# Twelve of 22 down-projection groups by Strassen instead of eleven, and seven of them prepared during the up projection instead of five

## The chip, the cores and the metric

The kernel runs on one core of a Trainium2 chip. Its metric is device time in microseconds. Three runs of the kernel before gave 1444.36, 1444.54 and 5140.6 us; the median, 1444.54 us, is what the prediction is compared with.

Five engines matter: TensorE (PE in the profile, with its weight loads as PEld), VectorE (DVE), ScalarE (ACT), and the queues from which DMAs are issued: SP's for nearly all of them, ACT's for a few. Every engine works through its own instructions strictly in the order in which they were written into the program; semaphores make one wait for another.

## The reference

One block of a streaming encoder on 256 tokens of width 2048, in float32: two token mixers (multi-scale mean pooling, multi-scale retention) merged by gates, and a gated feed-forward layer of width 5632. The change touches the feed-forward layer alone:

```python
def conv_glu(h, w_up, conv_w, conv_b, w_down):
    ug = h @ w_up                                  # (256, 2048) @ (2048, 11264)
    gate, up = ug[..., :D_FF], ug[..., D_FF:]      # D_FF = 5632
    gate = causal_depthwise_conv3(gate, conv_w) + conv_b
    return (jax.nn.silu(gate) * up) @ w_down       # (256, 5632) @ (5632, 2048)
```

## The kernel before

**Precision.** A float32 product is made of three matmuls on reduced-precision operands: each operand is split into a high part `hi` and a rest `lo`, and `mm3` (lines 106 to 108) adds hi*hi, lo*hi and hi*lo. A split is one ScalarE copy (line 98, writes `hi`) and one VectorE subtraction (line 99, writes `lo`). Weights come from memory into `raw` tiles (three buffers of 1 MB) and are split there into `hi` and `lo` tiles of 128x1024 (four buffers each), or into a larger tile `u` (18 buffers, called units).

**The up projection** is a loop of 44 steps, `j` = 0 to 43. A step loads two raw tiles (2 MB), splits them into four `hi` and four `lo` tiles, and multiplies: first 32 *wide* matmuls of 512 columns (line 967, they read `hi`), then 32 *narrow* ones of 256 columns (line 975, they read `lo`). The sums go into two PSUM tiles `acc`, one for the gate half and one for the up half. There are four `acc` tiles, so step j+2 uses the two of step j: it can't begin before they have been read. They are read by two ScalarE copies (line 990) and two VectorE additions (line 993); a row of some eight VectorE instructions behind these (995 to 1013) does the norm, the convolution and the gating, and writes the activations for the down projection, which stay on the chip.

**The down projection** is done in two passes (`p` = 0 and 1, one for each half of the output's columns) over 22 groups of 256 rows of `w_down`. A group is done in one of two ways. *Plain*: four blocks by two halves by `mm3`, 24 matmuls. *Strassen*: seven products of blocks, 21 matmuls, for which sums of weight blocks and sums of activation blocks are wanted. In before, groups 2, 4, 6, 8, 11, 12, 14, 17 and 18 (`STRASSEN`) get their activation sums in the up projection, in the step that finishes the group. Groups 9 and 15 (`LATE`) are kept as plain activations, and `form_late` makes their sums at the start of the down projection, when a unit has come free.

**Weight sums** are made in one of two places. `Pair.seven` makes them in the down projection (VectorE lines 339, 341 and 346, then four splits). For the groups in `PRE` (4, 9, 12, 15, 18), `prepare` makes them in the up projection: it loads the group's weights into a unit over SP's queue (line 293), makes the sums with three VectorE subtractions (310, 311, 312), and writes them back to memory over ACT's queue (line 940). `seven_prepared` then loads the sums (line 293 again) and three of the four raw blocks (line 945). Each group in `PRE` is prepared twice, once for each pass: ten calls, at steps j = 2, 5, 8, and so on.

**What sets the order.** A scheduler writes the order of each engine's queue when the program is built. It goes by priorities and its own estimate of when each operand will be there. Work on weights (`weights_first`) is put 128 places ahead, and results that free PSUM in the mixers (`results_first`) 64 places ahead; the evictions of the up projection (990, 993) carry no such mark. The page's names carry numbers that rise with the program text, so `acc_7516` and `acc_7517` are the two tiles of step 13 in the kernel before.

## Time and profile before

| | us |
|---|---|
| median of the runs | 1444.54 |
| the profiled execution's own time | 1445.01 |
| its span, first to last instruction | 1443.2 |
| PE busy (7126 matmuls) | 1433.7 (99%) |
| PEld busy | 1214.5 (84%) |
| DVE busy | 1228.1 (85%) |
| ACT busy | 812.9 (56%) |
| mean granted TensorE clock | 0.999 |

The up projection's 44 steps lie between about 720 and 1209.8 us of the span, the down projection between 1209.8 and 1435 us; the rest up to 1443 us is the last norm and the output. In the timeline a row gives the start, the length, the engine, the line, the operation with its operands, how often it stands there in a row, and in brackets how long the engine had been idle before and what ended that. An instruction's length can reach into the next one's: on VectorE one starts before the one before has ended.

### The profile page before, as it was taken

Reading aid. Unit: us, or ns where it says so; the run is one execution under the profiler, and the core shown is the slowest. Engines: PE = TensorE matmul, PEld = TensorE weight load, DVE = VectorE, ACT = ScalarE, POOL = GpSimd, SP = SyncE. Lnnn points to the kernel's source line nnn. Section 1 sums busy time; section 2 is a strip of 40 time slices with the busy share of each in tenths; the row PEclk is TensorE's granted clock in tenths of the full one; section 3 lists DMA queues with packets and bytes.
Section 4 is the critical chain, followed back from the end, with each engine's and each line's share of the span. In section 5 each row is a group of like instructions: output and inputs, shape, how many; then the busy total and the mean of one; then the engine's idle time right before and its main releaser. Section 6 shows DMA issues by size and latency. Waiting matters only on the chain.

```text
span 1443.2 us, 18861 instructions
## 1 busy us (share of the span) xinstructions
PE 1433.7 (99%) x7126; PEld 1214.5 (84%) x7126; DVE 1228.1 (85%) x1740; ACT 812.9 (56%) x1052; POOL 0.2 (0%) x4
## 2 busy tenths in 40 slices
PE   9999999999999999999999999999999999999997
PEld 7888888888888888888888888888888888888886
DVE  6887898889888898999978898778876878888887
ACT  6655655566655554555555545554555555666664
POOL 0000000000000000000000000000000000000000
PEclk9999999999999999999999999999999999999999
DMA  9555455456455656556667695567554455676774
GB/s 378 194 209 184 159 195 215 183 197 233 144 198 188 228 178 227 200 213 233 222 211 294 249 386 208 201 266 266 198 206 180 176 196 181 250 275 241 273 279 157
DMA packets 48043, 320.08 MB, mean 222 GB/s; under 512 B 5456, under 2 KB 6352, under 8 KB 11856
## 3 DMA queue, kind: packets, MB, share of 16 engines
q1 hardware_dynamic: 45936, 307.34, 58.4%
q10 hardware_dynamic: 2016, 11.54, 1.9%
q8 instruction: 56, 0.92, 0.3%
q14 instruction: 35, 0.29, 0.1%
HBM read 304.17 MB, written 14.68 MB: 221 GB/s over the span
## 4 chain that ended last, share of the span: by engine, by line
PE 98%; DVE 1%; ACT 0%; issue 0%; DVEq 0%
PE acc L967 22%; PE acc L106 15%; PE acc L108 15%; PE acc L107 15%; PE acc L975 12%; PE aux L106 6%; PE aux L107 6%; PE aux L108 6%; PE acc L447 0%; DVE lo L99 0%; PE aux L194 0%; PE aux L566 0%; PE aux L851 0%; PE aux L663 0%; PE aux L788 0%
## 5 line engine op out<-in xcount | busy, mean ns | idle before, releaser
L98 ACT ACTIVATE hi<-raw 128x1024 fp32r<-128x1024 f32 (+1 forms) x508 | 532.3, 1055 | 391.1 <-PE acc L107 156.0
L99 DVE TENSOR_TENSOR lo<-raw,hi 128x1024 fp32r<-128x1024 f32 (+1 forms) x508 | 601.4, 1216 | 114.5 <-ACT hi L98 72.3
L106 PE MATMUL acc<-hi,u 128*128 128x512 f32 x876 | 342.6, 391 | 0.1
L107 PE MATMUL acc<-hi,u 128*128 128x512 f32 x876 | 341.2, 390 | 0.0
L108 PE MATMUL acc<-lo,u 128*128 128x512 f32 x876 | 340.5, 389 | 0.0
L967 PE MATMUL acc<-u,hi 128*128 128x512 f32 x1408 | 328.2, 390 | 0.0
L967 PEld LDWEIGHTS acc<-u,hi 128*128 128x128 f32 x1408 | 261.3, 188 | 52.6 <-DVE u L103 0.2
L108 PEld LDWEIGHTS acc<-lo,u 128*128 128x128 f32 x876 | 164.4, 188 | 34.5 <-DVE lo L99 0.2
L106 PEld LDWEIGHTS acc<-hi,u 128*128 128x128 f32 x876 | 164.5, 188 | 34.4 <-DVE t L386 0.5
L107 PEld LDWEIGHTS acc<-hi,u 128*128 128x128 f32 x876 | 164.6, 188 | 33.2
L975 PEld LDWEIGHTS acc<-u,lo 128*128 128x128 f32 x1408 | 174.9, 192 | 3.5
L975 PE MATMUL acc<-u,lo 128*128 128x256 f32 x1408 | 176.0, 283 | 0.0
L106 PE MATMUL aux<-hi,u 128*128 128x512 f32 x260 | 101.6, 391 | 0.0
L107 PE MATMUL aux<-hi,u 128*128 128x512 f32 x260 | 101.2, 389 | 0.0
L108 PE MATMUL aux<-lo,u 128*128 128x512 f32 x260 | 101.0, 389 | 0.0
L990 ACT ACTIVATE t<-acc 128x256 f32<-128x256 f32 x88 | 33.2, 382 | 77.8 <-PE acc L975 77.7
L98 ACT ACTIVATE four<-raw 128x512 fp32r<-128x512 f32 x55 | 34.8, 632 | 65.9 <-DVE raw L346 42.3
L99 DVE TENSOR_TENSOR u<-u,u 128x1024 fp32r<-128x1024 f32 x57 | 69.5, 1219 | 1.3 <-ACT u L98 1.1
L98 ACT ACTIVATE u<-u 128x1024 fp32r<-128x1024 f32 x57 | 59.8, 1052 | 14.2 <-DVE u L339 13.0
L106 PEld LDWEIGHTS aux<-hi,u 128*128 128x128 f32 x260 | 48.8, 188 | 10.4 <-ACT hi L98 0.6
L108 PEld LDWEIGHTS aux<-lo,u 128*128 128x128 f32 x260 | 48.8, 188 | 10.2
L107 PEld LDWEIGHTS aux<-hi,u 128*128 128x128 f32 x260 | 48.8, 188 | 10.0
(219 smaller groups left out, 1264.2 us busy)
## 6 DMA issues: line engine op xcount, KB each, us to landing
raw<-in_w_up SPq DMA_DIRECT2D x88, 1024.0 KB, 5.4
raw<-in_w_in SPq DMA_DIRECT2D x85, 1024.0 KB, 4.8
raw<-in_w_down SPq DMA_DIRECT2D x34, 1024.0 KB, 4.9
raw<-in_w_ret_proj SPq DMA_DIRECT2D x16, 1024.0 KB, 4.9
raw<-in_w_out SPq DMA_DIRECT2D x16, 1024.0 KB, 4.9
u<-in_w_down SPq DMA_DIRECT2D x10, 1024.0 KB, 9.9
sums_out<-u ACTq DMA_DIRECT2D x10, 1024.0 KB, 5.4
u<-sums_out SPq DMA_DIRECT2D x10, 1024.0 KB, 6.7
```

What stands on the lines that cost most here:

```text
L98: act.activation(hi, src, AF.Copy)
L99: dve.tensor_tensor(lo, src, plain(hi), ALU.subtract)
L106: pe.matmul(o, ah, bh, start=start, stop=False)
L107: pe.matmul(o, al, bh, start=False, stop=False)
L108: pe.matmul(o, ah, bl, start=False, stop=stop)
L967: pe.matmul(o[half], w2[half][hf][0][:, i * P : (i + 1) * P], hview(kt), start=kt == 0, stop=False)
L975: pe.matmul(o[half][:, :T], wl, hview(kt)[:, :T], start=False, stop=kt == KT - 1)
L990: act.activation(small_part[:, half * T : (half + 1) * T], o[half][:, T:], AF.Copy)
```

## The change

Four things change. (1) Group lists: `STRASSEN` becomes 2, 3, 5, 6, 8, 11, 14, 17, 18 and `LATE` becomes 9, 12, 15, so that twelve groups go by Strassen in each pass instead of eleven. (2) `PRE` becomes 3, 6, 9, 12, 14, 15, 18: fourteen calls of `prepare` instead of ten, at every odd step j from 1 on instead of every third. (3) The late sums are made one group at a time, at groups 4, 7 and 10 of the first pass, instead of both at group 3. (4) The third late group's sums find no room in a unit; they are put into the places of four constants that are done with (`rb`, `vecs`, `ident`, `ones`) and into one of the seven small work tiles, which is held until group 15 of the second pass.

```diff
-STRASSEN = (2, 4, 6, 8, 11, 12, 14, 17, 18)
-LATE = (9, 15)
-PRE = (4, 9, 12, 15, 18)
+STRASSEN = (2, 3, 5, 6, 8, 11, 14, 17, 18)
+LATE = (9, 12, 15)
+PRE = (3, 6, 9, 12, 14, 15, 18)
...
     def sums(a11, a12, a21, a22, dst):
         st = t2k()
-        s1, s2, s3, s4 = (st[:, i * P : (i + 1) * P] for i in range(4))
+        sums_into([st[:, i * P : (i + 1) * P] for i in range(4)], a11, a12, a21, a22)
+        split(*dst, st)
+
+    def sums_into(dst, a11, a12, a21, a22):
+        s1, s2, s3, s4 = dst
         dve.tensor_tensor(s1, a21, a22, ALU.add)
...
     for j in range(NFF):
-        if j % 3 == 2 and todo_sums:
+        if j % 2 and todo_sums:
             prepare(*todo_sums.popleft())
...
-    def form_late():
+    late_room = []
+
+    def form_late(i):
+        g = LATE[i]
+        if i < 2:
+            late_room or late_room.append(unit(F32R))
+            dst = [late_room[0][:, (2 * i + j) * NB : (2 * i + j + 1) * NB] for j in range(2)]
+            late[g] = [[x[:, j * P : (j + 1) * P] for x in dst] for j in range(4)]
+        else:
+            r = [const.tile([P, n], F32R, tag=t, name=f"late_{t}") for t, n in (("rb", T), ("vecs", C_END))]
+            r += [const.tile([P, P], F32R, tag=t, name=f"late_{t}") for t in ("ident", "ones")]
+            x = t2k(512, F32R)
...
-            if p == 0 and g == 3:
-                form_late()
+            if p == 0 and g in (4, 7, 10):
+                form_late(g // 3 - 1)
```

The new lines move the lines below them by three or more, so that line 993 of the kernel before is line 996 of the changed one, 990 is 993, 967 is 970 and 975 is 978.

The order of the queues changes from step 3 of the up projection on; everything before stands as it did, and PE's own order is the same up to group 3 of the down projection. From there PE has six matmuls fewer. The prediction speaks of three places.

**VectorE around steps 13 to 15 of the up projection.** In the kernel before, `acc_7516` and `acc_7517` are step 13's sums, and the four `lo` tiles from 7635 to 7649 are step 14's weights:

```order
L1009 TENSOR_TENSOR t_7513<-t_7508,t_7502 128x128
L1010 TENSOR_TENSOR t_7513<-t_7508,t_7502 128x128
L99 TENSOR_TENSOR lo_7635<-raw_7632,hi_7634 128x1024
L99 TENSOR_TENSOR lo_7639<-raw_7632,hi_7638 128x1024
L99 TENSOR_TENSOR lo_7645<-raw_7642,hi_7644 128x1024
L99 TENSOR_TENSOR lo_7649<-raw_7642,hi_7648 128x1024
L993 TENSOR_TENSOR t_7603<-acc_7516,t_7602 128x256
L993 TENSOR_TENSOR t_7603<-acc_7517,t_7602 128x256
L995 TENSOR_TENSOR t_7603<-t_7603,rb 128x512
```

In the changed kernel `acc_7545` and `acc_7546` are step 13's sums, and the `lo` tiles from 7765 to 7779 belong to step 15; the last of step 14's `lo` tiles (7672) stands twelve rows above the first of these:

```order
L1013 TENSOR_TENSOR t_7536<-t_7531,t_7525 128x128
L311 TENSOR_TENSOR u_8177<-u_8177 128x512
L310 TENSOR_TENSOR u_8385<-u_8385 128x1024
L312 TENSOR_TENSOR u_8177<-u_8177 128x512
L311 TENSOR_TENSOR u_8385<-u_8385 128x512
L99 TENSOR_TENSOR lo_7765<-raw_7762,hi_7764 128x1024
L99 TENSOR_TENSOR lo_7769<-raw_7762,hi_7768 128x1024
L99 TENSOR_TENSOR lo_7775<-raw_7772,hi_7774 128x1024
L99 TENSOR_TENSOR lo_7779<-raw_7772,hi_7778 128x1024
L996 TENSOR_TENSOR t_7632<-acc_7545,t_7631 128x256
L996 TENSOR_TENSOR t_7632<-acc_7546,t_7631 128x256
```

The eviction of step 13 stood behind the splits of step 14; it now stands behind those of step 15, with preparations of later groups (lines 310 to 312) between. One step on it is the same, with one more row among the splits: step 14's eviction (`acc_7653`) behind step 16's splits.

```order
L99 TENSOR_TENSOR lo_7866<-raw_7863,hi_7865 128x1024
L99 TENSOR_TENSOR u_6093<-t_7646,u_6086 128x512
L99 TENSOR_TENSOR lo_7870<-raw_7863,hi_7869 128x1024
L99 TENSOR_TENSOR lo_7876<-raw_7873,hi_7875 128x1024
L99 TENSOR_TENSOR lo_7880<-raw_7873,hi_7879 128x1024
L996 TENSOR_TENSOR t_7740<-acc_7653,t_7739 128x256
L996 TENSOR_TENSOR t_7740<-acc_7654,t_7739 128x256
```

In all other steps of both kernels an eviction stands behind the splits of the next step, as in the first of these three pieces.

**PE at the start of step 15**, in the changed kernel; in the kernel before it reads the same but for the numbers:

```order
L978 MATMUL acc_7654<-u_5341,lo_7672 128x256 x4
L978 MATMUL acc_7654<-u_5342,lo_7672 128x256 x4
L970 MATMUL acc_7760<-u_5339,hi_7764 128x512 x4
L970 MATMUL acc_7760<-u_5340,hi_7764 128x512 x4
L970 MATMUL acc_7760<-u_5341,hi_7768 128x512 x4
```

`acc_7760` is the first tile of step 15 and takes the place of `acc_7545`. On PE nothing moved here.

**SP's queue at the start of the down projection.** In the kernel before, the sums of the first prepared group (4) are loaded behind the raw weights of groups 5 and 6:

```order
L288 DMA raw_10874<-in_w_down 128x2048
L945 DMA raw_10908<-in_w_down 128x1536
L288 DMA raw_10947<-in_w_down 128x2048
L288 DMA raw_10981<-in_w_down 128x2048
L293 DMA u_10910<-sums_out_4_6102 128x2048
```

In the changed kernel the first prepared group is 3, and its sums are loaded behind the raw weights of group 4:

```order
L288 DMA raw_10840<-in_w_down 128x2048
L948 DMA raw_10881<-in_w_down 128x1536
L288 DMA raw_10931<-in_w_down 128x2048
L293 DMA u_10883<-sums_out_3_6102 128x2048
L288 DMA raw_10965<-in_w_down 128x2048
```

The load of the sums stands one raw load behind that of the group's own blocks instead of two.

In SP's queue of the up projection the loads of `prepare` come closer together as well: between the second raw tile of step 11 and that of step 16 there are now eight of them beside ten raw tiles.

## The prediction

> **What bounds the kernel now.** I read the page first: which engine is busy, and who carries the chain that ended last.

> ```profile
> PE 1433.7 (99%) x7126; PEld 1214.5 (84%) x7126; DVE 1228.1 (85%) x1740; ACT 812.9 (56%) x1052; POOL 0.2 (0%) x4
> PE 98%; DVE 1%; ACT 0%; issue 0%; DVEq 0%
> ```

> PE is busy 99% of the span and is 98% of the chain. A busy share of pipelined matmuls proves little, so I looked next at what PE waited for (the view of waits, PE alone), and then at the chain in order of time, for three pieces of the up projection:

> ```profile
> PE aux L194 <- DVE warm L189: 1.2, 1, 1.2
> PE aux L107 <- DVE t L99: 0.2, 1, 0.2
> ...
> 1187.74 7.28 PE acc L967 x32
> 1195.02 3.83 PE acc L975 x32
> 1198.85 7.28 PE acc L967 x32
> ```

> PE waits 1.4 us in all. A step is 7.28 + 3.83 = 11.11 us of matmuls, and the next starts when it ends. So PE's own rate is the bound: a matmul taken away is time saved, and a hole made on PE is time lost, since no slack is left elsewhere on PE to win it back.

> VectorE is next. The busy time by stretch (columns: length, PE, PEld, DVE, ACT, POOL, clock, DMA share, GB/s) for an ordinary up step, for the fullest one, and for the first half of the down projection:

> ```profile
> 1187.70:1198.80 11.10, 11.10 (x66) 9.83 (x65) 8.15 (x13) 5.72 (x8) 0.00 (x0) 1.00 0.53 190
> 854.30:865.40 11.10, 11.10 (x66) 9.83 (x65) 11.06 (x19) 6.69 (x11) 0.00 (x0) 1.00 0.86 328
> 1210.00:1325.00 115.00, 114.99 (x506) 94.25 (x505) 101.61 (x121) 67.50 (x76) 0.00 (x0) 1.00 0.70 258
> ```

> VectorE has 3 us to spare in an ordinary up step and almost none in a step with preparations, and still PE does not stop. VectorE may be full; what counts is what stands where in its queue.

> **The change part by part.**

> *Six matmuls less.* One more group by Strassen in each pass: 24 - 21 = 3 matmuls, twice. One takes 7.28 / 32 = 0.2275 us from start to start, so 6 x 0.2275 = 1.37 us less on PE, all on the path. [...]

> *A small hole at the start of the down projection.* It is there now, at the first prepared group:

> ```profile
> 1232.91 0.39 PE L108 MATMUL acc<-four,u 128*128 128x512 f32 x1
> 1233.31 0.50 PE L106 MATMUL aux<-hi,u 128*128 128x512 f32 x1
> 1233.64 0.40 PE L107 MATMUL aux<-hi,u 128*128 128x512 f32 x1
> ...
> 1225.11 0.42 SPq L293 DMA_DIRECT2D u<-sums_out  x1
> ...
> 1232.19 1.06 ACT L98 ACTIVATE hi<-u 128x1024 fp32r<-128x1024 f32 x1 [2.22 <-DMA u<-sums_out]
> ```

> The steps of 0.40 and 0.33 us are 0.17 and 0.10 over the pace: 0.3 us, because the load of the sums stood behind two raw loads and ScalarE waited 2.22 us for it. With one raw load less ahead this goes: 0.3 us less. What is late next is VectorE, which must now serve groups 2, 3, 5 and 6 by Strassen beside the last up step and the late sums. The trace has no such row. Below, it costs nothing (VectorE had idle time around this place); above, all of a 2.22 us wait falls on PE. I take 0.3, nearer to what the same wait cost here.

> *Preparation and late sums.* Each of the four further calls costs VectorE the three rows below, 2.6 us, and the DMAs 2 MB:

> ```profile
> L310 DVE TENSOR_TENSOR u<-u 128x1024 f32<-128x1024 f32 x10 | 12.2, 1218 | 3.1 <-DMA u<-in_w_down 3.1
> L311 DVE TENSOR_TENSOR u<-u 128x512 f32<-128x512 f32 x10 | 6.8, 682 | 0.0
> L312 DVE TENSOR_TENSOR u<-u 128x512 f32<-128x512 f32 x10 | 6.8, 682 | 0.0
> ```

> In a step with 3 us of spare time that is free, apart from where the rows come to stand (below). In the down projection the twelve groups, seven of them prepared, want no more of VectorE than eleven with five prepared: a prepared group has no 339, 341 and 346. The third late group adds two additions, four sums and four small splits, some 3 us of VectorE in a stretch that leaves it 115 - 101.6 = 13.4 us idle; the constants whose places it takes were last read in the last up step, and of the seven work tiles six remain. I count all of this at zero; the cover is VectorE's idle time, and without it up to 3 us would fall on PE.

> *Two evictions that came to stand one step late.* This is the term that decides. In the changed queue step 13's two additions on `acc` stand behind the four splits of step 15, and step 14's behind those of step 16. The splits can't come early: a `lo` tile of step 15 takes the buffer of one of step 14 and waits until step 14's narrow matmuls have read it. And step 15's first matmul needs step 13's `acc` tile. So PE must finish step 14, and stand until VectorE has done the rest of the splits and one eviction. How long, an ordinary step shows (its narrow matmuls are the row from 1195.02, they end at 1198.85):

> ```profile
> 1196.01 4.63 DVE L99 TENSOR_TENSOR lo<-raw,hi 128x1024 fp32r<-128x1024 f32 x4 [0.89 <-PE acc L975]
> 1200.56 0.75 DVE L993 TENSOR_TENSOR t<-acc,t 128x256 f32<-128x256 f32 x2
> ...
> L993 DVE TENSOR_TENSOR t<-acc,t 128x256 f32<-128x256 f32 x88 | 33.6, 416 | 1.9 <-ACT t L990 1.9
> ```

> The splits start 0.99 us after the narrow matmuls, as soon as the first buffer is free; the first eviction starts at 1200.56 and is done 0.416 us later, at 1200.98, which is 2.13 us after the step's end. In before nobody waits for it then: the tile is wanted a whole step later. In the changed kernel PE waits for it. The second tile is done 0.34 us behind and is wanted half a wide stage later, so it costs nothing.

> Hole at step 15: at least 2.13 us. VectorE also comes late to it. The row-to-row times of a full stretch are

> ```profile
> 850.51 0.68 DVE L311 TENSOR_TENSOR u<-u 128x512 f32<-128x512 f32 x1
> 851.11 0.68 DVE L99 TENSOR_TENSOR u<-t,u 128x512 fp32r<-128x512 f32 x1
> 851.72 0.69 DVE L995 TENSOR_TENSOR t<-t,rb 128x512 f32<-128x512 f32 x1
> ...
> 853.18 1.22 DVE L310 TENSOR_TENSOR u<-u 128x1024 f32<-128x1024 f32 x1
> 854.32 1.22 DVE L99 TENSOR_TENSOR lo<-raw,hi 128x1024 fp32r<-128x1024 f32 x1
> ...
> 859.25 0.41 DVE L993 TENSOR_TENSOR t<-acc,t 128x256 f32<-128x256 f32 x1
> 859.59 0.47 DVE L1001 SCALAR_TENSOR_TENSOR t<-t,vecs,t 128x254 f32<-128x254 f32 x1
> ```

> 1.14 us for 1024 columns, 0.60 for 512, 0.34 for 256; for the others I estimate 0.20 to 0.48 by their size. From the first split of step 13 to that of step 14 the changed queue holds four splits (4.56 us) and two rows of 1024 columns, four of 512, one of 384, three of 256 and four smaller ones (2.28 + 2.40 + 0.48 + 1.02 + 0.9 = 7.1 us): 11.66, 0.5 us more than a step. From step 14's to step 15's it is four splits, two rows of 1024, five of 512, two of the convolution's and two small ones (4.56 + 2.28 + 3.0 + 0.8 + 0.4 = 11.0 us), so the delay is kept. The hole is 2.13 + 0.5 = 2.6 us. Hole at step 16: VectorE has an idle time ahead of it (6.3 us of rows against a longer step), so no delay is carried, but a row of 512 columns stands among the splits: 2.13 + 0.60 = 2.7 us. Together 5.3 us; without the delay and the row 4.3.

> *The DMAs of that stretch.* Queued on SP are eight loads beside ten raw tiles, and ScalarE's queue has the writes, each behind the subtraction that it waits for; behind such a write stand splits of the next step. In before a stretch with five loads went so:

> ```profile
> 815.00:865.00 50.00, 50.00 (x296) 44.56 (x295) 44.93 (x69) 24.59 (x35) 0.00 (x0) 1.00 0.95 375
> ...
> raw<-in_w_up SPq DMA_DIRECT2D x8, 1024.0 KB, 8.0
> sums_out<-u ACTq DMA_DIRECT2D x5, 1024.0 KB, 10.4
> u<-in_w_down SPq DMA_DIRECT2D x3, 1024.0 KB, 13.2
> ```

> 375 GB/s at a share of 0.95 is 395 at the full share: the DMA engines were full, and a raw tile took 8.0 us to land. In the changed kernel 26 transfers of 1.05 MB fall to five steps: 27.3 MB / 395 = 69 us against 55.6. What that costs PE no row shows. Below, nothing: raw tiles are asked for early. With three buffers a step's second raw tile takes the place of the first one of the step before, which is free after two splits, at 1196.01 + 2.3 = 1198.3 in the rows above, 0.5 us ahead of a step's end; its own matmuls come a step and half a wide stage later, 0.5 + 11.1 + 3.6 = 15 us. For the first raw tile it is 20 us. Above, all 13.4 us. I take 0.2, because in before PE waited for none of these; it's the open end of the range.

> The sum, against the profiled 1445.01: -1.4 - 0.3 + 0.3 + 5.3 + 0.2 = +4.1, that is 1449.1. The profiled execution is 0.47 above the median of the runs, so the median to expect is 1444.54 + 4.1 = **1448.6 us**. This is 0.3% and well inside the 2% that a measurement of this kernel can tell from no change.

> **The rivals.**

> *Not slower: the late evictions cost nothing* (a chance of 9%). VectorE would have to reach them before PE ends the step, because the splits do not in fact wait for the narrow matmuls' buffers. Then -1.4 - 0.3 + 0.5 gives 1443.3 us. Against it is the 0.89 us idle time above, which PE ended, and which the view of waits has in most up steps:

> ```profile
> DVE lo L99 <- PE acc L975: 34.8, 31, 2.5
> ```

> *The DMAs become the bound around steps 12 to 16* (12%). Then the stretch takes up to 13.4 us longer, in which the holes mostly hide: 1444.54 - 1.7 + 13.4 = 1456.2 us at the most, about 1453 if half of it is hidden. For it: 0.95 of the share is used already with five loads. Against: raw tiles come early, and each hole gives the DMAs time. It decides once raw tiles land later than some 14 us after their issue (15 less a ScalarE copy), against 8.0.

> *The holes slow PE's clock* (4%). The granted clock is 1.00 in all stretches shown, but PE's longest wait there is 1.2 us, so the trace has no gap like these. The mechanism here: after a hole of 2.6 us PE runs the next stretch at half pace. If that lasted as long as a wide stage half, 3.6 us, it would add 1.8 us per hole, 3.6 in all: 1452.2 us. [...]

> *Slower by over 2%*, 1473.4 us and more, would want 29 us. That is the DMA rival twice over; 1%.

> **How the numbers follow.** The forecast of two holes has 74%. Its own range goes from the low ends (-1.4 - 0.3 + 0 + 4.3 = +2.6: 1447.1) to the high ones (holes 5.3, 2.2 at group 3, 2 us of DMA wait: -1.7 + 9.5 = +7.8: 1452.3). To hold 8 in 10 it must take in the clock and nearly all of the DMA rival: up to 1455. Below I go to 1445.5, in case one of the two holes is half hidden (+1); the rival without holes is left out. Faster by over 2%: nothing here can do that, 1%. Slower by over 2%: 2% with what I have not thought of. The rest, 97%, is no change.

> **What would show each step.** In the changed kernel's waits of PE a row for `acc` of the up projection, line 970, waiting for VectorE's line 996, twice, 2.1 to 3 us each, in the stretch around steps 15 and 16 (885 to 905 us of the span); nothing like it in other steps. PE with 7120 matmuls in place of 7126. No steps of 0.40 us at the first prepared group, or other ones there of up to 2 us in total. An ordinary step still 11.11 us long. Wrong would be: no wait for line 996 and a shorter time (the eviction does not bind), waits for raw tiles or preparations in the same stretch (the DMAs), matmuls at twice the pace's time behind a hole (the clock), or holes in other up steps, which I expect nowhere.

## The result and the profile after

| | before | changed |
|---|---|---|
| time, median (lowest to highest) | 1444.49 us (1444.36 to 1444.54, and one run of 5140.6) | 1458.6 us (1457.82 to 1462.53) |
| ratio, with its 95% interval | 1 | 1.0101 [1.0086, 1.0115] |
| profiled execution, span | 1445.01, 1443.2 us | 1457.86, 1456.0 us |

The change is slower by 1.0%. The prediction was 1448.6 us with a range to 1455.0, so it named the sign and the bound of 2% rightly, and missed the size; the time lies above the range: +14.1 us in the medians, +12.8 us between the two profiled spans, where +4.1 was forecast.

The page of the changed kernel (busy time, then the chain that ended last), and what TensorE waited for (total, times, longest):

```profile
PE 1436.3 (99%) x7120; PEld 1215.7 (83%) x7120; DVE 1237.8 (85%) x1760; ACT 815.7 (56%) x1060; POOL 0.2 (0%) x4
PE 91%; DMA 4%; DVE 4%; issue 1%; ACT 0%; DVEq 0%; ACTq 0%; SPq 0%
...
PE acc L970 <- DVE t L996: 9.3, 2, 6.3
```

PE has its six matmuls less, and yet is busy 2.6 us longer. The row for line 996, twice, is new, and so are two waits of 0.5 us for a `lo` split (line 99) in the down projection. The timeline of PE around the row for line 996 (start, length, then in brackets the idle time before and what ended it):

```profile
883.53 3.99 PE L978 MATMUL acc<-u,lo 128*128 128x256 f32 x32
893.79 8.90 PE L970 MATMUL acc<-u,hi 128*128 128x512 f32 x32 [6.27 <-DVE t L996]
902.53 3.99 PE L978 MATMUL acc<-u,lo 128*128 128x256 f32 x32
909.58 9.14 PE L970 MATMUL acc<-u,hi 128*128 128x512 f32 x32 [3.05 <-DVE t L996]
918.55 4.00 PE L978 MATMUL acc<-u,lo 128*128 128x256 f32 x32
```

A step has 7.28 us of wide and 3.83 of narrow matmuls. Step 14 should hand over at 883.53 + 3.83 = 887.36; step 15 starts at 893.79: a hole of 6.43 us. Step 16 starts at 909.58 in place of 906.36: a hole of 3.22. And the two wide stages behind the holes take 8.74 and 8.97 us, 1.46 and 1.69 too much. 6.43 + 3.22 + 3.15 = 12.80, the whole difference of the spans. All else cancels: the stretch ahead came out 0.15 us shorter, the down projection 0.15 longer.

Why the long wide stages: busy time of PE, PEld, DVE, ACT and POOL in 4 us stretches, then the granted clock, the DMA share and GB/s:

```profile
888.00:892.00 4.00, 0.00 (x0) 0.00 (x0) 4.00 (x5) 2.14 (x3) 0.00 (x0) 0.74 1.02 430
892.00:896.00 4.00, 2.21 (x5) 1.82 (x6) 3.18 (x6) 0.41 (x2) 0.00 (x0) 0.50 1.02 428
896.00:900.00 4.00, 4.00 (x17) 3.27 (x16) 1.62 (x4) 1.06 (x1) 0.00 (x0) 0.91 1.02 424
...
908.00:912.00 4.00, 2.42 (x8) 1.95 (x9) 3.90 (x8) 0.00 (x0) 0.00 (x0) 0.80 0.92 352
912.00:916.00 4.00, 4.00 (x15) 3.22 (x14) 2.81 (x7) 2.29 (x3) 0.00 (x0) 0.77 0.38 154
```

The clock falls to half (0.50 from 892 to 896) in the first hole, and stays there for part of the wide stage behind it. Behind the second it falls 0.8 us after PE has started again: 0.80 over 4 us is 1.6 us at half, from 910.4 on. The DMA engines are full up to 900 us (a share of 1.02). And VectorE is full while PE stands (4.00 us of the 4 from 888 on):

```profile
861.06 1.23 DVE L310 TENSOR_TENSOR u<-u 128x1024 f32<-128x1024 f32 x1 [3.42 <-DMA u<-in_w_down]
...
865.72 4.63 DVE L99 TENSOR_TENSOR lo<-raw,hi 128x1024 fp32r<-128x1024 f32 x4
...
877.27 4.63 DVE L99 TENSOR_TENSOR lo<-raw,hi 128x1024 fp32r<-128x1024 f32 x4
...
888.69 4.62 DVE L99 TENSOR_TENSOR lo<-raw,hi 128x1024 fp32r<-128x1024 f32 x4
893.23 0.75 DVE L996 TENSOR_TENSOR t<-acc,t 128x256 f32<-128x256 f32 x2
```

Step 13's eviction (893.23) stands behind step 15's four splits, and PE goes on 0.56 us after it starts. On time, the splits would have begun 0.99 us after step 14's narrow stage, at 884.5; they began at 888.69, 4.2 us late. Some 27 us earlier VectorE had stood 3.42 us for a weight block to prepare, 7 us before that 0.77 for a ScalarE copy that waited for a raw tile, and it had hardly any idle time in between (0.30 us) to win that back.

VectorE's delay was not alone. The last raw tile of step 15 was late too, and ScalarE stood for it, with its own two reads of the accumulators behind (line 993):

```profile
889.86 1.06 ACT L98 ACTIVATE hi<-raw 128x1024 fp32r<-128x1024 f32 x1 [6.02 <-DMA raw<-in_w_up]
...
891.77 0.64 ACT L993 ACTIVATE t<-acc 128x256 f32<-128x256 f32 x2
```

This copy was done at 890.92, and VectorE's third split, which needs it, began at 888.69 + 2 x 1.14 = 890.97. So if step 15's splits had begun on time, they would have stood for this tile, and the eviction would have come no earlier. VectorE and the raw tile were late by the same time here; one profile can't say what either cost alone.

### The profile page after: what moved, and what is told of

It is laid out like the page before. It is cut to its first block, busy times and chain, and to the rows that moved or that the text cites. A ratio compares the mean times of both kernels' runs of the same rounds, so it can differ in the third digit from the quotient of the medians.

```text
span 1456.0 us, 18900 instructions
## 1 busy us (share of the span) xinstructions
PE 1436.3 (99%) x7120; PEld 1215.7 (83%) x7120; DVE 1237.8 (85%) x1760; ACT 815.7 (56%) x1060; POOL 0.2 (0%) x4
## 4 chain that ended last, share of the span: by engine, by line
PE 91%; DMA 4%; DVE 4%; issue 1%; ACT 0%; DVEq 0%; ACTq 0%; SPq 0%
PE acc L970 20%; PE acc L106 14%; PE acc L108 14%; PE acc L107 14%; PE acc L978 10%; PE aux L108 6%; PE aux L106 6%; PE aux L107 6%; DMA u<-in_w_down 2%; DVE lo L99 2%; DMA u<-sums_out 1%; DMA sums_out<-u 1%; DMA raw<-in_w_up 1%; PE acc L450 0%; DMA raw<-in_w_down 0%
## 5 line engine op out<-in xcount | busy, mean ns | idle before, releaser
L98 ACT ACTIVATE hi<-raw 128x1024 fp32r<-128x1024 f32 (+1 forms) x504 | 527.3, 1055 | 397.4 <-PE acc L107 155.6
L99 DVE TENSOR_TENSOR lo<-raw,hi 128x1024 fp32r<-128x1024 f32 (+1 forms) x504 | 597.5, 1216 | 107.5 <-ACT hi L98 72.0
L106 PE MATMUL acc<-hi,u 128*128 128x512 f32 x870 | 340.2, 391 | 0.1
L108 PE MATMUL acc<-lo,u 128*128 128x512 f32 x870 | 338.8, 389 | 0.5 <-DVE lo L99 0.5
L107 PE MATMUL acc<-hi,u 128*128 128x512 f32 x870 | 339.0, 390 | 0.0
L108 PEld LDWEIGHTS acc<-lo,u 128*128 128x128 f32 x870 | 163.3, 188 | 35.1 <-DVE lo L99 1.1
L106 PEld LDWEIGHTS acc<-hi,u 128*128 128x128 f32 x870 | 163.4, 188 | 34.2 <-DVE t L389 0.5
L107 PEld LDWEIGHTS acc<-hi,u 128*128 128x128 f32 x870 | 163.4, 188 | 32.9
L106 PE MATMUL aux<-hi,u 128*128 128x512 f32 x254 | 99.2, 390 | 0.0
L108 PE MATMUL aux<-lo,u 128*128 128x512 f32 x254 | 99.0, 390 | 0.0
L107 PE MATMUL aux<-hi,u 128*128 128x512 f32 x254 | 98.8, 389 | 0.0
L99 DVE TENSOR_TENSOR u<-u,u 128x1024 fp32r<-128x1024 f32 x59 | 71.9, 1219 | 7.4 <-ACT u L98 7.3
L993 ACT ACTIVATE t<-acc 128x256 f32<-128x256 f32 x88 | 32.9, 381 | 75.5 <-PE acc L978 75.5
L98 ACT ACTIVATE u<-u 128x1024 fp32r<-128x1024 f32 x59 | 62.0, 1054 | 22.5 <-DVE u L339 13.5
L98 ACT ACTIVATE four<-raw 128x512 fp32r<-128x512 f32 x57 | 36.0, 631 | 56.0 <-DVE raw L346 32.8
L108 PEld LDWEIGHTS aux<-lo,u 128*128 128x128 f32 x254 | 47.7, 188 | 10.4 <-DVE lo L99 0.5
L106 PEld LDWEIGHTS aux<-hi,u 128*128 128x128 f32 x254 | 47.7, 188 | 9.8 <-ACT hi L98 0.2
L107 PEld LDWEIGHTS aux<-hi,u 128*128 128x128 f32 x254 | 47.7, 188 | 9.7
## 6 DMA issues: line engine op xcount, KB each, us to landing
raw<-in_w_up SPq DMA_DIRECT2D x88, 1024.0 KB, 6.1
raw<-in_w_in SPq DMA_DIRECT2D x85, 1024.0 KB, 4.8
raw<-in_w_down SPq DMA_DIRECT2D x30, 1024.0 KB, 5.3
raw<-in_w_ret_proj SPq DMA_DIRECT2D x16, 1024.0 KB, 4.9
raw<-in_w_out SPq DMA_DIRECT2D x16, 1024.0 KB, 4.9
u<-in_w_down SPq DMA_DIRECT2D x14, 1024.0 KB, 11.2
sums_out<-u ACTq DMA_DIRECT2D x14, 1024.0 KB, 9.1
u<-sums_out SPq DMA_DIRECT2D x14, 1024.0 KB, 7.0
```

Of the source, the lines that this page charges most:

```text
L98: act.activation(hi, src, AF.Copy)
L99: dve.tensor_tensor(lo, src, plain(hi), ALU.subtract)
L106: pe.matmul(o, ah, bh, start=start, stop=False)
L107: pe.matmul(o, al, bh, start=False, stop=False)
L108: pe.matmul(o, ah, bl, start=False, stop=stop)
L993: act.activation(small_part[:, half * T : (half + 1) * T], o[half][:, T:], AF.Copy)
```

## The experiments

Three theories. **A**: the place of the evictions behind the splits makes the holes; late loads and the clock only lengthen them. **B**: the loads of the stretch starve the splits, and PE would stand without any late eviction. **C**: VectorE has too much to do there. All ratios are to the kernel before on the same chip, with 95% intervals.

| run | median us | ratio | span us |
|---|---|---|---|
| e1_evict_first | 1444.75 | 0.9998 [0.9989, 1.0007] | 1442.3 |
| e2_prepare_only | 1444.7 | 0.9997 [0.9988, 1.0006] | 1442.1 |
| e3_groups_only | 1451.4 | 1.0046 [1.0032, 1.0059] | 1448.6 |
| e4_spread | 1454.8 | 1.0074 [1.0058, 1.0090] | 1454.1 |
| e5_quiet_defer | 1454.96 | 1.0068 [1.0053, 1.0084] | 1452.6 |
| e6_quiet_dense | 1470.77 | 1.0178 [1.0164, 1.0192] | 1469.4 |
| e7_no_sums | 1451.55 | 1.0043 [1.0030, 1.0057] | 1450.8 |
| e8_evict_first_g4 | 1446.04 | 1.0008 [0.9999, 1.0017] | 1443.7 |
| e9_store_1408 | 1454.22 | 1.0065 [1.0048, 1.0082] | 1451.2 |
| e10_store_1280 | 1452.21 | 1.0051 [1.0036, 1.0066] | 1450.9 |
| e11_quiet_again | 1456.53 (one run) | | 1454.8 |
| e12_after_again | 1463.74 (one run) | | 1462.0 |

**Take the place away: e1.** The changed kernel, with the two copies and two additions that read `o[half]` put ahead in the scheduler's priority:

```diff
-        for half in range(2):
-            act.activation(small_part[:, half * T : (half + 1) * T], o[half][:, T:], AF.Copy)
-        for half in range(2):
-            h2 = slice(half * T, (half + 1) * T)
-            dve.tensor_tensor(gu[:, h2], o[half][:, :T], small_part[:, h2], ALU.add)
+        with tc.high_priority(offset=300):
+            ...
```

> The changed kernel with one edit: the two ScalarE copies and two VectorE additions that read a step's sums in the up projection are given priority, so that they stand ahead of the next step's splits in both queues. The work and the DMAs are those of the changed kernel; the loads of the preparations still stand eight in five steps. Theory A (the place of the evictions makes the two holes; late DMAs and the clock only lengthen them): no wait of PE for an eviction, clock 0.999, and the six matmuls less show: 1444.5 - 1.4 to 1444.5 - 0.4, so 1443.1 to 1444.1 us. Theory B (the DMAs of that stretch starve the splits): PE still stands there, now for splits, 4 us or more in all: 1447 us or more. Theory C (VectorE has more work in that stretch than it can do): the same as B, without ScalarE's waits for raw tiles.

The 1% is gone, and PE's waits have no row for the eviction any more. But the loads were as late as before. VectorE (line 997 is the eviction here) and then PE, steps 14 to 16:

```profile
858.74 1.23 DVE L310 TENSOR_TENSOR u<-u 128x1024 f32<-128x1024 f32 x1 [2.96 <-DMA u<-in_w_down]
...
882.10 0.74 DVE L997 TENSOR_TENSOR t<-acc,t 128x256 f32<-128x256 f32 x2
...
886.96 2.36 DVE L99 TENSOR_TENSOR lo<-raw,hi 128x1024 fp32r<-128x1024 f32 x2
889.70 2.36 DVE L99 TENSOR_TENSOR lo<-raw,hi 128x1024 fp32r<-128x1024 f32 x2 [0.39 <-ACT hi L98]
...
886.76 7.44 PE L970 MATMUL acc<-u,hi 128*128 128x512 f32 x32
894.04 4.00 PE L978 MATMUL acc<-u,lo 128*128 128x256 f32 x32
```

VectorE still stood 2.96 us for a weight block, and step 15's splits began at 886.96, after PE had begun step 15. It didn't matter: a `lo` tile is wanted at the narrow stage, at 894.04, 7.28 us into the step. An eviction is wanted when its tile's next step begins. That is the difference between the two kinds of VectorE row, and why the order between them decides. The time is the kernel before's within 0.1%, not the 1 us less that the six matmuls promise; that is taken up below (e8).

**Take the groups away, keep the loads: e2.** The kernel before with the seven prepared groups, called every second step:

```diff
-PRE = (4, 9, 12, 15, 18)
+PRE = (4, 6, 9, 12, 14, 15, 18)
-        if j % 3 == 2 and todo_sums:
+        if j % 2 and todo_sums:
```

> The kernel before with one part of the change: its own eleven groups, but seven of them prepared (4, 6, 9, 12, 14, 15, 18), at every odd step. The fourteen loads come as closely as in the changed kernel (ten of them by step 13), but no eviction stands behind the splits of the step after next. Theory A: no hole, 1444.5 us within 0.7. Theory B: the loads alone cost PE several us, 1450 us or more. Theory C: as B.

No change. In its order no eviction stands behind the splits two steps on. So the denser loads and VectorE's preparations alone cost nothing, against B and C.

**Fewer preparations, with one eviction displaced: e3 and e4.** e3 is the changed kernel with the five preparations and the schedule of before; e4 the changed kernel with all seven, called every third step. The first diff is e3's alone, the second that of both:

```diff
-PRE = (3, 6, 9, 12, 14, 15, 18)
+PRE = (3, 9, 12, 15, 18)
```

```diff
-        if j % 2 and todo_sums:
+        if j % 3 == 2 and todo_sums:
```

> The changed kernel with five preparations for each pass (3, 9, 12, 15, 18) at every third step: the new groups alone. The loads are ten as in the kernel before, but the scheduler puts one eviction, step 13's, behind the splits of step 15. [...] Theories B and C: no hole, since the load on the DMAs and on VectorE is that of the kernel before: 1443.1 to 1444.1 us.

> The changed kernel with its fourteen preparations called at every third step instead of every second: five loads stand around step 13 as in the kernel before, the others later. One eviction (step 13's) stands late. Theory A: one hole of 2.1 to 3.5 us as with the groups alone, 1445.2 to 1447.6 us. Theory B: at most as much as the kernel before, no hole: 1443.1 to 1444.1 us. Theory C: as B.

In both, step 13's eviction stands behind step 15's splits, step 14's does not. Step 15 of e3, then of e4:

```profile
890.27 9.15 PE L970 MATMUL acc<-u,hi 128*128 128x512 f32 x32 [2.43 <-DVE t L996]
```

```profile
890.85 9.12 PE L970 MATMUL acc<-u,hi 128*128 128x512 f32 x32 [2.74 <-DVE t L996]
```

One displaced eviction, one hole, as A says. Both times are above the 1445.2 to 1447.6 us that A gave for either, for two reasons. The wide stage behind the hole was too long, which my numbers left out (e3: the narrow stage began at 899.26, so the wide one took 8.99 us, 1.71 too much; behind the holes of the changed kernel, at a clock of 0.50, it was 1.46 and 1.69). And in e4 the last preparations fell behind the up projection, so that the down projection stood 1.68 and 2.88 us for its first prepared groups (at 1232.09 and 1237.33). Calling them later only moves the trouble.

e3 also shows what keeps a delay alive. Its VectorE stood for a block as well, and yet its hole is a bare one:

```profile
871.49 1.22 DVE L310 TENSOR_TENSOR u<-u 128x1024 f32<-128x1024 f32 x1 [2.70 <-DMA u<-in_w_down]
...
878.18 4.62 DVE L99 TENSOR_TENSOR lo<-raw,hi 128x1024 fp32r<-128x1024 f32 x4
...
885.17 4.62 DVE L99 TENSOR_TENSOR lo<-raw,hi 128x1024 fp32r<-128x1024 f32 x4
```

The splits of step 14 began 4.45 us late (878.18; on time is 0.99 us after the narrow stage of step 13, which began at 872.74), those of step 15 only 0.33 us late (885.17 against 884.84). Between the two groups stand 2.4 us of other rows. In the changed kernel it is 6.9 us (881.8 to 888.69), most of them rows of further preparations, and the delay stays. So a late block doesn't lengthen a hole by itself; it does where VectorE's queue is too full to win the time back. That points to C's part in the cost: not the holes, but their length.

**Put the place into the kernel before, where nothing else goes on: e5.** The rest of an up step from its eviction on is made a function, and for steps 27, 33 and 39 it is written two steps later:

```diff
+        w2 = [load_split(ins["w_up"][2 * j + half]) for half in range(2)]
+        if j in deferred:
+            tail(*deferred.pop(j))
         o = [acc_tile() for _ in range(2)]
-        w2 = [load_split(ins["w_up"][2 * j + half]) for half in range(2)]
...
+        if j in (27, 33, 39):
+            deferred[j + 2] = (j, o)
+        else:
+            tail(j, o)
```

> The kernel before, with nothing but the place of three evictions changed: the two additions that read the accumulators of up steps 27, 33 and 39 are written two steps later, so that on VectorE they stand behind the lo-splits of steps 29, 35 and 41. No preparation runs there (its loads stand at steps 4 to 26), and no load is added. Theory A (the place of an eviction makes the hole): three holes of TensorE at steps 29, 35 and 41, each 2.0 to 2.8 us of waiting for line 'gu = ...' (the eviction), each with 0 or 1.4 to 1.8 us of half clock behind it, so 6 to 14 us above the kernel before: 1451 to 1459 us. Theory B (late loads starve the splits): no load is late, TensorE waits for nothing, the time stays within 1 us of the kernel before. Theory C (VectorE has too much to do): VectorE has the same work, so no change either.

Three holes at the three steps (line 963 is the eviction, 1002 the wide stage, 1010 the narrow one):

```profile
1039.49 3.99 PE L1010 MATMUL acc<-u,lo 128*128 128x256 f32 x32
1045.72 7.55 PE L1002 MATMUL acc<-u,hi 128*128 128x512 f32 x32 [2.24 <-DVE t L963]
...
1114.90 9.16 PE L1002 MATMUL acc<-u,hi 128*128 128x512 f32 x32 [2.23 <-DVE t L963]
...
1185.70 7.55 PE L1002 MATMUL acc<-u,hi 128*128 128x512 f32 x32 [2.24 <-DVE t L963]
```

This is the bare price of one displaced eviction: 2.24 us of waiting, or 1045.72 - (1039.49 + 3.83) = 2.40 from start to start. VectorE's rows from 1034 to 1050 us have no wait for a load, and an ordinary step leaves VectorE a quarter of its time (8.15 us busy of 11.10 in the kernel before), so B and C would have given nothing. Shown: the place alone makes a hole. One of three equal holes was followed by half clock: behind the second, the clock was 0.52, 0.50, 0.50 and 0.77 in the four microseconds from 1116 on, and the wide stage 1.7 us longer than 7.28; behind the first it was 1.00.

**The same with dense loads: e6.** e5, with the ten preparations of the kernel before moved to one per step from step 25 on:

```diff
-        if j % 3 == 2 and todo_sums:
+        if j >= 25 and todo_sums:
```

> As e5_quiet_defer, with the same three evictions behind the splits, but the ten preparations of the kernel before are called one per step from step 25 on, so that their loads and stores stand at steps 23 to 32: around the hole of step 29, and not around those of steps 35 and 41. If late loads only lengthen a hole that the place of the eviction makes (theory A with the lateness that the trace of after suggests): the hole at step 29 is 3 to 7 us, those at 35 and 41 stay as in e5_quiet_defer, and the time is 0.5 to 5 us above it. If the place alone sets the hole: the same three holes, the time within 0.7 us of e5_quiet_defer. Theory B: the hole at 29 alone, none at 35 and 41.

The waits at steps 27, 29, 30 and 35:

```profile
1028.13 7.54 PE L1002 MATMUL acc<-u,hi 128*128 128x512 f32 x32 [3.07 <-DVE t L963]
...
1058.00 8.95 PE L1002 MATMUL acc<-u,hi 128*128 128x512 f32 x32 [6.58 <-DVE t L963]
1073.42 9.16 PE L1002 MATMUL acc<-u,hi 128*128 128x512 f32 x32 [2.64 <-DVE t L963]
...
1133.10 7.55 PE L1002 MATMUL acc<-u,hi 128*128 128x512 f32 x32 [2.24 <-DVE t L963]
```

Steps 35 and 41 (2.24 as well), away from the loads, are as in e5 to a hundredth. Step 29, with the same displaced eviction among the loads, went from 2.24 to 6.58 us. That is the lengthening, at the size seen in the changed kernel (6.27). The time is above my range, though. At step 30 PE waited for step 28's eviction, which the scheduler had put behind step 30's splits (VectorE has the splits at 1068.00 and the eviction at 1072.95), so e6 has four displaced evictions and not three. PE also stood at steps 27 (3.07 us) and 28 (0.56), whose evictions are in their place, and 2.12 us for a ScalarE copy at step 26. Ahead of the eviction that step 27 waited for, VectorE itself had stood 5.42 us for a block; ahead of the copy, ScalarE had stood 5.81 us for a raw tile. So with a preparation in each step late loads alone make holes, as B has it. The changed kernel, by e1 and e2, is below that density. Whether the deferral had a part in these waits wasn't tried.

**Lighten VectorE, keep the loads: e7.** The changed kernel without the sums of the preparation:

```diff
     def prepare(p, g):
         raw = load_unit(ins["w_down"][p * (NFF // 2) + g])
-        weight_sums(raw)
         act.dma_start(sums_out[p, g], raw)
```

> The changed kernel with the sums of the weights left out of the preparation (the block is loaded and stored as it is, so the prepared groups' products are not the reference's): all its DMAs stay, VectorE has 14 x (1.23 + 0.68 + 0.68) = 36 us less to do in the up projection. In its order the evictions of steps 11 and 12 stand behind the splits of steps 13 and 14. Theory A: two holes at steps 13 and 14 of 2.0 to 2.8 us, with 0 or 1.4 to 1.8 us of half clock behind each, on top of 1443.1 to 1444.5: 1447 to 1453 us. Theory C (VectorE's load): no hole in the up projection, 1443 to 1444.5 us. Theory B (loads starve the splits): holes wherever a split waits for raw, not for the eviction; 1446 to 1460 us.

VectorE was busy 1207.6 us, 30 less than in the changed kernel, and still (line 995 is the eviction here):

```profile
867.06 9.15 PE L969 MATMUL acc<-u,hi 128*128 128x512 f32 x32 [2.33 <-DVE t L995]
...
882.32 7.52 PE L969 MATMUL acc<-u,hi 128*128 128x512 f32 x32 [2.27 <-DVE t L995]
```

Two holes at steps 13 and 14, where this kernel's order has its two displaced evictions, of the bare size: with no sums, VectorE waits for no weight block, and the holes aren't lengthened. So it isn't VectorE's work that makes the holes, and the place costs 2.3 us of waiting each. Which part of the rest comes from late blocks and which from VectorE's full queue, e7 can't tell: it takes both away, and the evictions displaced in it are those of other steps.

**Fewer bytes stored: e9 and e10.** The changed kernel, storing 1408 (e9) or 1280 (e10) of a prepared block's 2048 columns:

```diff
-        act.dma_start(sums_out[p, g], raw)
+        act.dma_start(sums_out[p, g][:, :1408], raw[:, :1408])
-        rt = load_unit(sums_out[p, g])
+        rt = load_unit(ins["w_down"][p * (NFF // 2) + g])
```

> The changed kernel with 1408 of the 2048 columns of each prepared block stored (0.69 MB instead of 1 MB), and the plain block read back in its place (prepared products are then not the reference's; as many bytes are read as before). In the order both halves of step 14's eviction and the second half of step 13's stand behind the splits two steps on, as in the changed kernel. If the place makes the hole and the queueing of DMAs lengthens it: two holes again; the first, 6.3 us of waiting in the changed kernel, comes to 3 to 5.5 us, as five stores fewer by 0.31 MB each leave 1.6 MB or 4 us less to move at 400 GB/s in that stretch; the second 2.2 to 3.2 us; with 1.4 to 1.8 us of half clock behind one or both: 1450 to 1457 us. If the first hole's length has nothing to do with the DMAs: 6 us again, 1456.5 to 1459 us.

> As e9_store_1408 with 1280 columns stored (0.63 MB). TensorE's and SyncE's orders are word for word those of e9, and the DMAs differ by 0.06 MB a store; but on VectorE both halves of step 13's eviction now stand ahead of the splits of step 15, and only step 14's stands behind those of step 16. Theory A (place): the hole at step 15 is gone, the one at step 16 stays with 2.2 to 3.2 us of waiting and 0 or 1.4 to 1.8 us of half clock: 1446 to 1450.5 us, 3 to 7 us below e9. Theory B (late loads starve the splits): the same DMAs give the same holes; within 1 us of e9.

PE from step 15 on in e9, and step 16 in e10:

```profile
887.83 3.81 PE L970 MATMUL acc<-u,hi 128*128 128x512 f32 x16
891.89 3.89 PE L970 MATMUL acc<-u,hi 128*128 128x512 f32 x16 [0.25 <-DVE t L996]
...
904.66 9.14 PE L970 MATMUL acc<-u,hi 128*128 128x512 f32 x32 [5.04 <-DVE t L996]
```

```profile
903.10 9.63 PE L970 MATMUL acc<-u,hi 128*128 128x512 f32 x32 [4.19 <-DVE t L996]
```

The places come out as A has them: in e9 only the second half of step 13's eviction is displaced, and PE runs the first half of step 15 and stands 0.25 us in its middle; in e10 neither half is, and PE stands nowhere in step 15 (32 matmuls from 887.63 in 7.44 us). I had not seen that half a displacement costs next to nothing. The sizes are misses: the hole at step 16 came out longer than in the changed kernel (5.04 and 4.19 against 3.05), so the two kernels differ by 2.0 us where 3 to 7 were expected. Here VectorE's own rows did it. From 860 to 902 us it stood idle for 0.25 us in e9 and 0.04 us in e10, so it waited for next to no load. It came to step 16's splits 1.23 and 1.27 us late (897.84 and 897.17; on time are 896.61 and 895.90), and 1.69 and 0.78 us of other rows stood among them. With the bare hole of 2.40 that makes 5.3 and 4.5 us; from start to start the holes are 5.21 and 4.36. Before 860 VectorE had stood 2.59 and 1.70 us for a block; whether it would have been late without that isn't shown. How the first hole's length goes with the bytes stored stays open, since the edit moved the eviction too.

**A version faster than both? e8.** e1's six matmuls less should have shown as 1.37 us. Its down projection has new waits: 0.7 us for a ScalarE copy and 0.5 for a `lo` split at prepared group 3 of the second pass, whose sums landed late. e8 prepares group 4 in its place:

```diff
-STRASSEN = (2, 3, 5, 6, 8, 11, 14, 17, 18)
-PRE = (3, 6, 9, 12, 14, 15, 18)
+STRASSEN = (2, 4, 5, 6, 8, 11, 14, 17, 18)
+PRE = (4, 6, 9, 12, 14, 15, 18)
```

> e1_evict_first with group 4 in the place of group 3 among the Strassen and the prepared groups. In e1 the second pass of the down projection had waits of 0.7 and 0.5 us (1.8 us from start to start) at group 3, whose sums landed late behind the change of passes. Theory A: no hole in the up projection, and at group 4 the sums have one group more to land: those 1.8 us go, 1442.8 to 1444.2 us, ratio 0.9980 to 0.9993. If the wait only moves to group 4 or another: as e1, 1444.2 to 1445.2 us.

The wait left the second pass and came up in the first: 0.30 us at 1233.43 and 0.46 us at 1243.63, both for a ScalarE copy. At 1.0008 it is no better. No version here beats the kernel before; e1 undoes the loss.

**The same kernels once more: e11 and e12.** e5's and the changed kernel's code, profiled again.

> e5_quiet_defer once more, unchanged, to see what of a hole is the program's and what is not. If the place of the evictions sets the holes: again three, 2.2 us of waiting each, within 0.1 us. [...] If the clock falls by the place in the program: behind the second hole again, and only there.

> The changed kernel once more, unchanged. [...]

The three holes of e11, then the two of e12:

```profile
1045.10 9.16 PE L1002 MATMUL acc<-u,hi 128*128 128x512 f32 x32 [2.24 <-DVE t L963]
1115.89 7.55 PE L1002 MATMUL acc<-u,hi 128*128 128x512 f32 x32 [2.24 <-DVE t L963]
1185.08 9.17 PE L1002 MATMUL acc<-u,hi 128*128 128x512 f32 x32 [2.24 <-DVE t L963]
```

```profile
894.45 10.35 PE L970 MATMUL acc<-u,hi 128*128 128x512 f32 x32 [6.84 <-DVE t L996]
911.50 10.37 PE L970 MATMUL acc<-u,hi 128*128 128x512 f32 x32 [2.88 <-DVE t L996]
```

The holes repeat: in e11 to a hundredth, in the changed kernel within 0.6 us. e11's span, 1454.8, is the 1443.2 of the kernel before, three bare holes (7.2), two wide stages too long by 1.7 each and a wait of 0.7 us in the down projection: 1454.5. The clock does not repeat: in e5 the second wide stage was long, in e11 the first (its clock 0.75, 0.50, 0.50 and 0.54 in the four microseconds from 1046 on) and the third. The program and the length of the holes were the same, so neither settles which hole is followed by half clock. In e12 both wide stages are long by 2.9 us (10.35 and 10.37 against 7.44), and a wait in the second pass of the down projection was followed by a lower clock too (0.59 on the mean from 1358 to 1362 us); its 1463.74 us is 2.7 above the 1461 that I allowed at most.

## Why the prediction was right and wrong

**Bound and mechanism: right.** PE's rate is the bound, VectorE is next, and what counts is the order in VectorE's queue. The sign, the two steps (15 and 16), the waiting line (970) and the line waited for (996) came out as written. e1 and e5 show it from both sides: with the place removed the loss goes, and with the place alone put in there are holes.

**The bare hole: nearly right.** 2.13 us were worked out from the rows of an ordinary step; e5 has 2.40. For two holes that is 0.5 us too little.

**The failed step: "The DMAs of that stretch ... I take 0.2".** Together with the delay of 0.5 and the row of 0.6 among the splits, the prediction had VectorE 1.3 us late in all. Measured: 6.43 + 3.22 - 2 x 2.40 = 4.85, or 3.55 more. Step 16 has 0.82 of it, near the 0.6 for the row; step 15 has 4.03 where 0.5 and 0.2 were forecast. The bound from above (13.4 us) was there; the choice near its low end was made because in before PE waited for none of these loads, and because raw tiles have 15 to 20 us of slack.

Both reasons follow a load straight to PE, and the way went through VectorE. It stood 3.42 us for a block to prepare, at `L310`, and from there its splits began late: by 3.42 us in step 13, 3.86 in step 14 and 4.17 in step 15 (865.72, 877.27 and 888.69, against 0.99 us after the start of each narrow stage before). In before (3.1 us in two waits at `L310`), and in e1 (2.96), such a wait is absorbed by a `lo` tile's slack; with the eviction behind the splits the same delay goes through to PE. The raw tile's slack shrank in the same way: with the eviction displaced, what counts is not the tile's own matmuls but its `lo` split, ahead of the eviction. In the second profile of the changed kernel (e12) VectorE stood for that tile's copy:

```profile
888.45 2.35 DVE L99 TENSOR_TENSOR lo<-raw,hi 128x1024 fp32r<-128x1024 f32 x2
891.61 2.36 DVE L99 TENSOR_TENSOR lo<-raw,hi 128x1024 fp32r<-128x1024 f32 x2 [0.80 <-ACT hi L98]
```

There the wait for the block was shorter (2.23 us, and 1.07 for the next), and the hole longer (6.84). So late loads of both kinds, of blocks and of a raw tile, made up what was forecast at 0.2, with a VectorE too full to win the time back. How the 4 us divide between them stays open.

The two terms were not independent, and I added them as if they were. I had also worked out that "the delay is kept" from step to step, and that came out (11.55 and 11.42 us from first split to first split, worked out as 11.66 and 11.0), but I had not asked which delays there would be.

**The clock: a rival at 4%, and it happened.** 3.15 us in the first profile, about 5.8 in e12. The prediction priced it at 3.6 and gave it 4%, the author's estimate: the trace of before, where PE's longest wait is 1.2 us, shows nothing for or against so low a chance. Here 2.24 us of waiting were enough, once of three times in e5 and twice of three in e11, and the wide stage behind then took 1.7 us too much; in the other three it took 0.1 too much. No run shows a length of hole below which the clock holds. Holes and clock together should have been the likeliest case.

**Preparation and late sums at zero, and the small hole: wrong together by 1.4 us.** The six matmuls, the hole at 1232.9 and group 3 were to give -1.4. The six matmuls are gone (7120). But the down projection (from 1222.45 to the end, 233.55 us; before from 1209.80, 233.40) is no shorter:

```profile
1299.74 0.40 PE L107 MATMUL aux<-hi,late_ident 128*128 128x512 f32 x1
1300.64 0.50 PE L108 MATMUL aux<-lo,late_vecs 128*128 128x512 f32 x1 [0.50 <-DVE lo L99]
...
1352.67 0.40 PE L107 MATMUL acc<-hi,u 128*128 128x512 f32 x1
1353.60 0.50 PE L108 MATMUL acc<-lo,u 128*128 128x512 f32 x1 [0.53 <-DVE lo L99]
```

Two waits for `lo` splits of prepared groups, 0.90 and 0.93 us from start to start where 0.23 is the pace, ate the gain. The first is at the third late group, but its late sums aren't shown to be the cause: ScalarE had stood 1.78 us there for the load of the weight sums, and VectorE's split came behind that. That the small hole went is right; two others came.

The terms, predicted and measured: bare holes 4.3 and 4.8; VectorE's lateness 1.3 and 4.85; clock 0 and 3.15; the rest -1.4 and 0.0. Together 4.2 (4.1 in the prediction, which rounds its two holes to 5.3) and 12.8.

**The rivals.** That late evictions cost nothing is refuted by the changed kernel and e5. That the DMAs become the bound came nearest in time (1453 to 1456.2, against 1458.6), but not as it was written: the DMA engines were full (424 to 430 GB/s at a share of 1.02), and in e1, just as full (404 to 442 GB/s in slices of 1.5 us from 852 to 897), PE waited for none of it. Here the loads lengthened a hole that the order had made; they made none. Its sign, raw tiles that land later than 14 us after their issue, was set too far out: in e12 step 15's last tile, issued at 878.71, held up the splits when it landed some 12 us later.

## What to carry to other kernels

Ask of every row in a full engine's queue when its result is wanted: a row wanted at once (freeing an accumulator) must not stand behind rows wanted seven microseconds later; in e5 that cost 2.40 us a time with a quarter of VectorE's time free. A delay that was harmless (2.96 us in e1) becomes costly (4.03 us at step 15) once such a row stands behind it and the queue has no room to win it back, so a displaced row and a busy stretch are to be priced together, not added. And a hole on TensorE should be priced with the half clock behind it: here 1.7 us more behind three of the six holes of 2.24 us in e5 and e11.

## What the hardware showed unasked

```profile
890.00:891.00 1.00, 0.00 (x0) 0.61 1.05 442
891.00:894.00 3.00, 0.00 (x0) 0.50 1.01 421
894.00:897.00 3.00, 2.55 (x6) 0.50 1.01 429
...
900.00:901.00 1.00, 1.00 (x5) 0.77 0.97 410
```

(PE alone here: length, busy, clock, DMA share, GB/s.) With the rows between 1.00 and 0.50 taken as a mixture of the two, a clock of 0.61 over one microsecond is 0.78 us at half, and 0.77 is 0.46 us: half clock from 890.2 to 900.5, 10.2 us. PE was busy again from 894.45, and the clock stayed at half for 6 us more. In the first profile's rows above, 0.74, 0.50 and 0.91 over 4 us each make 2.1 + 4.0 + 0.7 = 6.8 us at half, and 0.80 and 0.77 make 1.6 + 1.8 = 3.4. Around the first hole of both profiles the clock fell while PE stood (at 889.9 and 890.2), behind the second of the first profile 0.8 us after PE had started again. What sets these lengths and moments is not shown.
